# Step sizes, first norm and last block of a two-layer trunk: three changes of order in one kernel

## The chip, the cores and the metric

The kernel runs on one core of a Trainium2 chip. The metric is the device time of one execution in microseconds, the lower the better. The core has a matrix engine (PE, with its weight loads PEld), a vector engine (DVE), a scalar engine (ACT), a general engine (POOL) and a queue for transfers (SP). Each executes its own instructions in order and waits for others by semaphores.

## What is computed

The reference is a decoder trunk of two layers on 256 positions of width 2048, everything in float32:

```python
h = _mamba2_mixer(x, ...)              # layer 0
x = _layernorm(ALPHA * x + h, ln_g[0], ln_b[0])
k, v = _shared_kv(x, kv_w, kv_b, cos, sin)
h = _swa_mixer(x, k, v, ...)           # layer 1
x = _layernorm(ALPHA * x + h, ln_g[1], ln_b[1])
```

The mixer of layer 0 projects `x` to gates, values, B, C (8 groups) and step sizes (64 heads), convolves over time, and forms for each group decays `exp(-(sum of dt * a))`, which are multiplied into the products of C and B. The step sizes are `dt = softplus(dt_raw + bias)`, and the decays need their running sums over time. The outcome is gated, normalized by group and projected by `w_out`. Layer 1 is an attention over a window of 128 with one shared set of keys and values, projected from the normalized `x`; its own outcome is gated, projected by `w_out` and added to the normalized `x`, before the second norm.

## The kernel before, in words

**Weights.** All weights come in units of 128 x 2048 (`srcs`, the list of all of them in the order of use). A unit is loaded in two halves on SP's queue (`wr<-in_wa` and the like, L130) and each half is split into a high part (`wh`, ACT, L139) and the rest (`wl`, DVE, L140), so that a product in float32r of three matmuls gives float32's exactness: high by high, high by low, low by high (`mac`, L216; `out_unit`, L272; `x_stat`, L776). `next_unit` (L211) loads two units ahead of the one in use; there are four buffers each for the high and the low parts.

**Order.** A planner orders each engine's instructions at build time, from its own estimates of their durations and from the order in which the program issues them; `tc.keep_in_program_order(m)` takes the instruction `m` out of this freedom, and `tc.high_priority(n)` moves a stretch ahead. Work that belongs to a later step is called through `plan`, a list by step (`at(t, fn)`, ten steps for a group of layer 0), or in layer 1 through `later(n, fn)`, which calls it `n` ticks later; a tick follows each weight unit.

**Start.** `first_products` (L313) loads `x` transposed, unit 0 and the step sizes' weights in pieces (`FIRST`), and issues the products in the order of `ORDER`: entry 0 is the raw step sizes (L326, small float32 products), entries 1 and 2 are the products of units 0 and 1. `make_dt` (L338) then forms the step sizes in two functions. `first` (L344) has the bias, the absolute value and the exponential on ACT, and on DVE the reciprocal and the start of a polynomial for log(1 + e); `second` (L359) has eight polynomial steps (L362 to L364), `da = dt * a` and its rounding into a high and a low part (L368 to L371), two running sums (L374), and the transfer of the sums to a buffer in memory (`rscr`, L387). The calls are: load unit 2; `first`; load unit 3 with its DVE splits pinned; `second`; load unit 4 with its DVE splits pinned (L621 to L625). `turn_dt` (L393, step `TD`) transposes the sums. `load_decay` (L431) spreads rows of `rscr` over all partitions (`rb`), `sum_decay` (L451) subtracts and clips them on ACT into `e` (L459, eight operations for each half of a group), `exp_decay` (L464) applies the exponential, `by_cb` (L502) multiplies by the products of C and B on DVE. For group 0 the steps are `TS` for the first `sum_decay` and `TS + 1`, `TS + 2` for the rest.

**First norm.** `out_last` (L289) has the last group's output products (four blocks of 512 columns, two halves `h` of the positions), adds them to `xr` on DVE (L285) and takes statistics (L709). `done1(h)` (L726) follows each half: mean and variance (L713), Ln and Exp for the reciprocal deviation (L715, L716), and then for each chunk of 512 columns two operations on DVE (L731, L734) that also apply gain and shift from `gb`, spread over the partitions; four transposes of 128 on PE into one PSUM tile (L739); the high part `x1H` on ACT (L744), the low part `x1L` on DVE (L745). The keys and values (`x_stat`, L781 to L783) take `x1H` and `x1L`, chunk by chunk, for half 0 and then half 1.

**End.** The same `out_last` is used for layer 1 with `done2` (L977). For half 1 the second norm's last step is divided: for two chunks DVE subtracts the mean and multiplies by the gain (L992), PE adds the shift by a product of a row of ones with one row of the shift (L985) and multiplies by the reciprocal deviation as a diagonal matrix `dg` (L996), ACT copies and issues the transfer (L997, L998); for the other two DVE does both steps (L992, L1000) and SP issues the transfer.

Of the kernel before, what the change touches and what calls it, by code (L numbers as in the profile page):

```python
# [16 lines left out]
P = 128  # L17
# [11 lines left out]
TD, TS, CB0 = 3, 4, 8  # L29
# [3 lines left out]
ORDER = [(0, 0, 1), (1, 0, 2), (0, 1, 4), (1, 2, 6), (0, 4, 8), (1, 6, 8), (2, 0, 8), (0, 8, 14), (1, 8, 14),  # L33
         (0, 14, 16), (1, 14, 16), (2, 8, 16)]
# [12 lines left out]
           ("q", 3), ("g", 3), ("o", 2), ("o", 3)]  # L47
ALPHA = (2.0 * 2) ** 0.25
# [16 lines left out]
def trunk(ctx: ExitStack, tc: tile.TileContext, A: dict, out: bass.AP, dbg=None):  # L65
# [134 lines left out]
    def load_next(n, pin=False):  # L200
        for _ in range(n):
            if len(units) == 4:
                nc.sync.dma_start(cc[:], A["cc"])
            if len(units) in XK_AT:
                i = XK_AT.index(len(units))
                v = xr[:, i // 2, i % 2 * 1024 : i % 2 * 1024 + 1024]
                nc.sync.dma_start(v, A["xk"][:, i // 2, i % 2 * 1024 : i % 2 * 1024 + 1024])
                nc.scalar.activation(v, v, AF.Copy, scale=ALPHA)
            units.append(load_unit(srcs[len(units)], BROKEN if len(units) in broken else [WHOLE, WHOLE], pin))
# [62 lines left out]
    def out_unit(aH, aL, h, u, nb, first, rms=None):  # L272

        ps = mm_tile()
        hs = slice(h * P, (h + 1) * P)
        for k in range(4):
            ks = slice(k * 512, (k + 1) * 512)
            nc.tensor.matmul(ps[:], aH[:, k, hs], u.h[:, ks], start=k == 0, stop=False)  # L278
            nc.tensor.matmul(ps[:], aL[:, k, hs], u.h[:, ks], start=False, stop=False)  # L279
            nc.tensor.matmul(ps[:], aH[:, k, hs], u.l[:, ks], start=False, stop=k == 3)  # L280
        v = xr[:, h, nb * 512 : (nb + 1) * 512]
        if first:
            nc.vector.scalar_tensor_tensor(v, v, ALPHA, ps[:], ALU.mult, ALU.add)
        elif rms is not None:
            nc.vector.scalar_tensor_tensor(v, ps[:], rms[:, h : h + 1], v, ALU.mult, ALU.add)  # L285
        else:
            nc.vector.tensor_tensor(v, v, ps[:], ALU.add)

    def out_last(aH, aL, rms, stats, done):  # L289

        us = []
        for nb in range(4):
            us.append(next_unit())
            out_unit(aH, aL, 0, us[nb], nb, False, rms)
            stats(0, nb)
            if nb == 0:
                out_unit(aH, aL, 1, us[nb], nb, False, rms)
                stats(1, nb)
        done(0)
        for nb in range(1, 4):  # L300
            out_unit(aH, aL, 1, us[nb], nb, False, rms)
            stats(1, nb)
# [35 lines left out]
    def make_dt(ps):  # L338
# [3 lines left out]
        bias = pc[:, PC_DTB : PC_DTB + 1]  # L342

        def first():  # L344
            tc.keep_in_program_order(nc.vector.tensor_scalar(u, ps[:, :P], bias, None, ALU.add))
            nc.scalar.activation(e, ps[:, :P], AF.Abs, bias=bias)
            nc.scalar.activation(e, e, AF.Exp, scale=-1.0)
            aneg = ap.tile([P, 1], F32, tag="aneg", name="aneg")
# [7 lines left out]
            tc.keep_in_program_order(nc.vector.tensor_scalar(q, w, 1.0 / 15.0, None, ALU.mult))  # L356
            return aneg

        def second(aneg):  # L359
# [4 lines left out]
            tc.keep_in_program_order(ops.scalar_tensor_tensor(dt, u, 0.0, q, ALU.max, ALU.add))  # L364
            sums = f[4][:].rearrange("p (k t) -> p k t", k=2)
# [85 lines left out]
    def sum_decay(g, hf):  # L451
# [4 lines left out]
        for h in range(4):  # L456
            for c, cols in ((0, slice(0, 256)), (1, slice(256, 384))):

                nc.scalar.activation(  # L459
                    e[:, h, cols], rb[:, h, c * P :], AF.Relu, scale=-1.0, bias=rtk[:, c, h0 + h : h0 + h + 1]  # L460
                )
        es[g, hf] = e
# [158 lines left out]
    load_next(1)  # L621
    aneg = dt_first()
    load_next(1, True)
    dts = dt_second(aneg)
# [40 lines left out]
    for g in range(NG):  # L665
# [13 lines left out]
        else:  # L679
# [28 lines left out]
    def norm_stats(st, h, nb):  # L708
        nc.vector.bn_stats(st[:, h, nb, :], xr[:, h, nb * 512 : (nb + 1) * 512])  # L709

    def norm_scale(lp, st, h):
        mv = lp.tile([P, 2], F32, tag="mv", name=nm("mv"), bufs=2)
        nc.vector.bn_aggr(mv[:], st[:, h, :, :])  # L713
# [5 lines left out]
    with ExitStack() as s2:  # L719
        lp = pool("lp", stack=s2)  # L720
        gb = lp.tile([P, 2, D], F32, tag="gb", name="gb1")
        nc.gpsimd.dma_start(gb[:, 0, :], A["lng"][0].partition_broadcast(P))
        nc.gpsimd.dma_start(gb[:, 1, :], A["lnb"][0].partition_broadcast(P))
        st1 = lp.tile([P, 2, 4, 6], F32, tag="st", name="st1")

        def done1(h):  # L726
            mv, rs = norm_scale(lp, st1, h)
            for c in range(4):
                sl = slice(c * 512, (c + 1) * 512)
                t = lp.tile([P, 512], F32, tag="t", name=nm("t"), bufs=2)  # L730
                nc.vector.scalar_tensor_tensor(  # L731
                    t[:], xr[:, h, sl], mv[:, 0:1], gb[:, 0, sl], ALU.subtract, ALU.mult
                )
                nc.vector.scalar_tensor_tensor(  # L734
                    xr[:, h, sl], t[:], rs[:], gb[:, 1, sl], ALU.mult, ALU.add
                )
                ps = ax_tile()
                for k in range(4):
                    nc.tensor.transpose(  # L739
                        ps[:, k * P : (k + 1) * P], xr[:, h, c * 512 + k * P : c * 512 + (k + 1) * P], ident  # L740
                    )
                dst = (slice(None), slice(c * 4, c * 4 + 4), slice(h * P, (h + 1) * P))
                psv = ps[:].rearrange("p (k t) -> p k t", k=4)
                nc.scalar.activation(x1H[dst], psv, AF.Copy)  # L744
                nc.vector.tensor_tensor(x1L[dst], psv, x1H[dst].bitcast(F32), ALU.subtract)  # L745

        if PRE:
            tc.keep_in_program_order(nc.scalar.preload_act_table_set("natural_log_exp_and_others"))
        out_last(*gs[NG - 1].y, gs[NG - 1].rms, lambda h, nb: norm_stats(st1, h, nb), done1)
# [26 lines left out]
    def x_stat(ps, h, u, ui):  # L776
        for k in range(4):
# [3 lines left out]
            nc.tensor.matmul(ps[:], x1H[:, kk, hs], u.h[:, ks], start=kk == 0, stop=False)  # L781
            nc.tensor.matmul(ps[:], x1L[:, kk, hs], u.h[:, ks], start=False, stop=False)  # L782
            nc.tensor.matmul(ps[:], x1H[:, kk, hs], u.l[:, ks], start=False, stop=kk == KT - 1)  # L783
# [6 lines left out]
    for h in range(2):  # L790
        ps = mm_tile()
        for ui in range(4):
            if h == 0:
                kv_u.append(next_unit())
            x_stat(ps, h, kv_u[ui], ui)
# [17 lines left out]
        later(2, ktr)  # L813

# [160 lines left out]
    st2 = bp.tile([P, 2, 4, 6], F32, tag="st", name="st2")  # L975

    def done2(h):  # L977
        mv, rs = norm_scale(bp, st2, h)
        if h:

            dg = bp.tile([P, P], F32, tag="dg", name="dg")
            pss = [ax_tile(), ax_tile()]
            for c in range(2):
                sl = slice(c * 512, (c + 1) * 512)
                nc.tensor.matmul(pss[c][:], ones[0:1, :], gb2[1][0:1, sl], start=True, stop=False)  # L985
            nc.scalar.activation(dg[:], ident, AF.Copy, scale=rs[:])
            for c in range(4):
                sl = slice(c * 512, (c + 1) * 512)
                v = xr[:, h, sl]
                o = out[h * P : (h + 1) * P, sl]  # L990
                t = bp.tile([P, 512], F32, tag="pt", name=nm("t"), bufs=4)
                nc.vector.scalar_tensor_tensor(  # L992
                    t[:], v, mv[:, 0:1], gb2[0][:, sl], ALU.subtract, ALU.mult
                )
                if c < 2:
# [111 lines left out]
```

## Time and profile before

| | us |
|---|---|
| median of 3 runs | 1017.23 |
| lowest and highest | 1015.32, 1019.07 |
| the profiled execution | 1016.18 |
| its span in the trace | 1014.4 |
| PE, DVE, ACT busy | 999.1, 764.3, 558.5 |
| DVE splits of weights (L140) | 398.8 in 342 instructions |
| ACT splits of weights (L139) | 338.0 in 342 instructions |
| weights and other data moved | 198.79 MB |

An engine's busy time is the time in which one of its instructions ran. Matmuls overlap, and the profile models their ends, so for PE the distance from one start to the next is more telling than the busy time. A row of a timeline gives start, duration, engine, line, operation, output and input, and in brackets how long the engine was idle ahead of it and who ended that. A row of the table by stage gives a stretch and for each engine its busy time and number of instructions, then the granted clock of PE as a share, the share of the DMA engines and GB/s. A row of the waits gives the total, the number and the longest.

### The profile page before, as it was taken

What the parts mean: (1) busy time and instruction counts of PE and PEld (TensorE: products, weight loads), DVE (VectorE), ACT (ScalarE), POOL (GpSimd) and SP (SyncE); (2) the same over time, 40 slices, a digit from 0 to 9 for tenths busy, and PEclk for the clock granted to TensorE, in tenths of its full rate; (3) what the DMA queues carried; (4) which work ended last, traced back from release to release, by engine and by line L of the source; (5) the groups of instructions that cost most, each with busy time, mean ns of one, the idle gap of its engine ahead of it and who ended that gap; (6) DMA issues with size and microseconds to landing.
All of it is one profiled execution on the core that took longest, in us unless ns stands there. A gap on an engine that the chain in (4) does not pass through costs nothing.

```text
span 1014.4 us, 17615 instructions
## 1 busy us (share of the span) xinstructions
PE 999.1 (98%) x7011; PEld 900.2 (89%) x7011; DVE 764.3 (75%) x1109; ACT 558.5 (55%) x926; POOL 93.1 (9%) x116
## 2 busy tenths in 40 slices
PE   8999999999999999999999999999999999999997
PEld 7999899999998998999999999877988878879975
DVE  5679987877786787686786687798577775775786
ACT  5595847637655655664654764534554543543642
POOL 0100303004003002100300300401000000000002
PEclk9999999999999999999999999999999999999998
DMA  9896666575666666666656556646655545545532
GB/s 333 274 298 202 206 239 200 169 227 170 221 214 188 223 194 205 202 191 201 206 174 230 149 189 219 238 143 233 191 181 161 158 151 179 176 147 182 175 118 83
DMA packets 57858, 198.79 MB, mean 196 GB/s; under 512 B 6368, under 2 KB 10608, under 8 KB 57264
## 3 DMA queue, kind: packets, MB, share of 16 engines
q1 hardware_dynamic: 55648, 189.91, 57.9%
q0 software_dynamic: 1520, 7.10, 2.0%
q8 instruction: 55, 0.90, 0.4%
q10 hardware_dynamic: 608, 0.66, 0.2%
q14 instruction: 27, 0.22, 0.1%
HBM read 195.41 MB, written 2.23 MB: 195 GB/s over the span
## 4 chain that ended last, share of the span: by engine, by line
PE 82%; DVE 8%; ACT 3%; DMA 3%; issue 2%; POOL 1%; SPq 0%; ACTq 0%; POOLq 0%; DVEq 0%
PE mm L218 44%; PE mm L278 7%; PE mm L279 7%; PE mm L280 7%; PE mm L781 3%; PE mm L782 3%; PE mm L783 3%; DVE wl L140 2%; PE ax L537 2%; ACT wh L139 2%; PE ax L873 1%; PE ax L931 1%; DVE cv L419 1%; DMA wr<-in_wo 1%; DMA rb<-rscr 1%
## 5 line engine op out<-in xcount | busy, mean ns | idle before, releaser
L140 DVE TENSOR_TENSOR wl<-wr,wh 128x1024 fp32r<-128x1024 f32 (+2 forms) x342 | 398.8, 1183 | 135.7 <-ACT wh L139 133.8
L139 ACT ACTIVATE wh<-wr 128x1024 fp32r<-128x1024 f32 (+2 forms) x342 | 338.0, 1011 | 229.4 <-PE mm L218 74.3
L218 PE MATMUL mm<-xH,wh 128*128 128x256 f32 x1280 | 356.7, 279 | 1.7 <-DVE cv L419 1.3
L218 PE MATMUL mm<-xH,wl 128*128 128x256 f32 x1280 | 355.4, 278 | 1.3 <-DVE wl L140 1.3
L218 PE MATMUL mm<-xL,wh 128*128 128x256 f32 x1280 | 355.4, 278 | 0.0
L218 PEld LDWEIGHTS mm<-xH,wh 128*128 128x128 f32 x1280 | 241.2, 188 | 4.6 <-issue 2.4
L218 PEld LDWEIGHTS mm<-xH,wl 128*128 128x128 f32 x1280 | 241.1, 188 | 2.0 <-DVE wl L140 1.9
L218 PEld LDWEIGHTS mm<-xL,wh 128*128 128x128 f32 x1280 | 241.2, 188 | 1.0
L278 PE MATMUL mm<-wh,yH 128*128 128x512 f32 x256 | 101.4, 396 | 0.0
L279 PE MATMUL mm<-wh,yL 128*128 128x512 f32 x256 | 99.9, 390 | 0.0
L280 PE MATMUL mm<-wl,yH 128*128 128x512 f32 x256 | 99.7, 390 | 0.0
L553 POOL TENSOR_TENSOR yz<-yz,z 128x256 f32<-128x256 f32 x32 | 32.9, 1035 | 521.4 <-DVE yz L548 521.4
L419 DVE SCALAR_TENSOR_TENSOR cv<-mm,pc,cv 128x255 f32<-128x255 f32 x144 | 68.8, 478 | 8.3 <-ACT cv L417 6.9
L218 PE MATMUL mm<-x1H,wh 128*128 128x256 f32 x256 | 71.9, 281 | 0.0
L218 PE MATMUL mm<-x1H,wl 128*128 128x256 f32 x256 | 71.0, 277 | 0.0
L218 PE MATMUL mm<-x1L,wh 128*128 128x256 f32 x256 | 71.0, 277 | 0.0
L781 PE MATMUL mm<-wh,x1H 128*128 128x512 f32 x160 | 63.3, 396 | 0.0
L782 PE MATMUL mm<-wh,x1L 128*128 128x512 f32 x160 | 62.7, 392 | 0.2 <-DVE x1L L745 0.2
L783 PE MATMUL mm<-wl,x1H 128*128 128x512 f32 x160 | 62.6, 391 | 0.2 <-DVE wl L140 0.2
L278 PEld LDWEIGHTS mm<-wh,yH 128*128 128x128 f32 x256 | 48.1, 188 | 10.3 <-DVE z L490 1.0
L280 PEld LDWEIGHTS mm<-wl,yH 128*128 128x128 f32 x256 | 48.1, 188 | 10.2
L279 PEld LDWEIGHTS mm<-wh,yL 128*128 128x128 f32 x256 | 48.1, 188 | 9.0
(186 smaller groups left out, 1298.4 us busy)
## 6 DMA issues: line engine op xcount, KB each, us to landing
wr<-in_wa SPq DMA_DIRECT2D x158, 512.0 KB, 5.0
wr<-in_wo SPq DMA_DIRECT2D x64, 512.0 KB, 4.3
wr<-in_wq SPq DMA_DIRECT2D x32, 512.0 KB, 4.6
wr<-in_wg SPq DMA_DIRECT2D x32, 512.0 KB, 4.5
wr<-in_wb SPq DMA_DIRECT2D x32, 512.0 KB, 4.6
rb<-rscr SPq DMA_DIRECT2D x14, 512.0 KB, 5.1
wr<-in_wkv SPq DMA_DIRECT2D x8, 512.0 KB, 6.1
el<-rscr SPq DMA_DIRECT2D x14, 256.0 KB, 4.7
```

What stands on the lines that cost most here:

```text
L139: nc.scalar.activation(h[:, sl], v, AF.Copy)
L140: m = nc.vector.tensor_tensor(l[:, sl], v, h[:, sl].bitcast(F32), ALU.subtract)
L218: m = nc.tensor.matmul(ps, a, b, start=first and i == 0, stop=last and i == 2)
L278: nc.tensor.matmul(ps[:], aH[:, k, hs], u.h[:, ks], start=k == 0, stop=False)
L279: nc.tensor.matmul(ps[:], aL[:, k, hs], u.h[:, ks], start=False, stop=False)
L280: nc.tensor.matmul(ps[:], aH[:, k, hs], u.l[:, ks], start=False, stop=k == 3)
L419: nc.vector.scalar_tensor_tensor(a[:, sft:], ps[:, : S - sft], w(3 - sft), a[:, sft:], ALU.mult, ALU.add)
L537: nc.tensor.matmul(ps[64 * r : 64 * r + 64, cols], xd[:, c, r, :], e[:, 256:] if c else e[:, :256], start=c == 0, stop=c == 1,)
L553: nc.gpsimd.tensor_tensor(v, v, st.z[i][:], ALU.mult)
L781: nc.tensor.matmul(ps[:], x1H[:, kk, hs], u.h[:, ks], start=kk == 0, stop=False)
L782: nc.tensor.matmul(ps[:], x1L[:, kk, hs], u.h[:, ks], start=False, stop=False)
L783: nc.tensor.matmul(ps[:], x1H[:, kk, hs], u.l[:, ks], start=False, stop=kk == KT - 1)
```

## The change

1. **Step sizes.** In `ORDER` the small products of entry 0 from piece 8 to 16 come in one stretch, ahead of entry 1's; before, pieces 14 and 15 came in a second stretch. The chain is cut into three functions, with the DVE splits of units 2, 3 and 4, now all pinned, around them. The pins of the first function fall away. `TS` becomes 5. For groups 0 and 1 the `sum_decay` operations are pinned on ACT, the second half's `sum_decay` and `exp_decay` come one step later, and its `by_cb` as well. The loads of `xk` are pinned on SP's queue.
2. **First norm.** The norm is split: `center` subtracts the mean and divides by the deviation, alternating by chunk between DVE and ACT; the chunks are transposed, and gain and shift are applied after the transposition, where they are a column per partition (`gbc`, a new small input), four operations of 128 columns for each chunk, alternating between ACT and DVE. The transposes come in pairs of chunks, at fixed places in PE's order: half 0 among the last output products, half 1 among the keys' products. Output products and the keys' products of half 0 are pinned. Since `xr` now lacks gain and shift, `residual` applies them later, two DVE operations for each chunk and half, at ticks 1 to 4 and 9 to 12 of layer 1, with gain and shift loaded for each chunk.
3. **End.** In the last block of half 1 the product, the addition and the statistics come in two halves of 256 columns. The shift is added by a product of the identity with the shift spread over all partitions, and `dg` takes two and a half chunks in place of two.

```diff
-TD, TS, CB0 = 3, 4, 8
+TD, TS, CB0 = 3, 5, 8
-ORDER = [..., (2, 0, 8), (0, 8, 14), (1, 8, 14), (0, 14, 16), (1, 14, 16), (2, 8, 16)]
+ORDER = [..., (2, 0, 8), (0, 8, 16), (1, 8, 16), (2, 8, 16)]
+RES_AT = [1, 2, 3, 4, 9, 10, 11, 12]
...
-    load_next(1)
-    aneg = dt_first()
+    dt_first()
     load_next(1, True)
-    dts = dt_second(aneg)
+    dt_sums = dt_second()
+    load_next(1, True)
+    dts = dt_sums()
     load_next(1, True)
...
+        wide = g < 2
         at(steps, sum_decay, g, 0)
         at(steps + 1, exp_decay, g, 0)
-        at(steps + 1, sum_decay, g, 1)
-        at(steps + 2, exp_decay, g, 1)
+        at(steps + 1 + wide, sum_decay, g, 1)
+        at(steps + 2 + wide, exp_decay, g, 1)
         at(t + pos["cb"], cb, g)
         for hf in range(2):
-            at(t + pos["cb"] + hf * (g > 1), by_cb, g, hf)
+            at(t + pos["cb"] + hf, by_cb, g, hf)
...
+    def center(h):
+        mv, rs = norm_scale(lp, st1, h)
+        nmr = lp.tile([P, 1], F32, tag="nmr", name=nm("nmr"), bufs=2)
+        nc.vector.tensor_scalar(nmr[:], mv[:, 0:1], rs[:], -1.0, ALU.mult, ALU.mult)
+        for c in range(4):
+            v = xr[:, h, c * 512 : (c + 1) * 512]
+            if c % 2:
+                nc.scalar.activation(v, v, AF.Identity, scale=rs[:], bias=nmr[:])
+            else:
+                nc.vector.tensor_scalar(v, v, mv[:, 0:1], rs[:], ALU.subtract, ALU.mult)
+    def turn_x1(h, c, tp, tag, bufs):
+        ps = ax_tile()
...
+        for k in range(4):
+            v, g_, b_ = ps[:, k * P : (k + 1) * P], *[gbc[:, i, c * 4 + k : c * 4 + k + 1] for i in range(2)]
+            if c % 2:
+                nc.vector.tensor_scalar(x1[:, k, :], v, g_, b_, ALU.mult, ALU.add)
+            else:
+                nc.scalar.activation(x1[:, k, :], v, AF.Identity, scale=g_, bias=b_)
+        nc.scalar.activation(x1H[dst], x1, AF.Copy)
+        nc.vector.tensor_tensor(x1L[dst], x1, x1H[dst].bitcast(F32), ALU.subtract)
+    for h, nb in ((0, 0), (1, 0), (0, 1), (0, 2), (0, 3), (1, 1), (1, 2), (1, 3)):
+        if h == 0:
+            us[nb] = next_unit()
+        out_unit(*yHL, h, us[nb], nb, False, rms, True)
+        norm_stats(st1, h, nb)
+        if nb == 3:
+            center(h)
+        for c in {(1, 2): (0, 1), (1, 3): (2, 3)}.get((h, nb), ()):
+            turn_x1(0, c, x1p, "x1", 2)
...
+            x_stat(ps, h, kv_u[ui], ui, h == 0)
+            if h == 0:
+                for c in ((), (), (0, 1), (2, 3))[ui]:
+                    turn_x1(1, c, bp, "pt", 4)
...
+    def residual(c, h):
+        if h == 0:
+            for i, n in enumerate(("lng", "lnb")):
+                gb1[i] = bp.tile([P, 512], F32, tag=f"gb{i}", name=nm("gb1"), bufs=1)
+                nc.gpsimd.dma_start(gb1[i][:], A[n][0, c * 512 : (c + 1) * 512].partition_broadcast(P))
+        v = xr[:, h, c * 512 : (c + 1) * 512]
+        tc.keep_in_program_order(nc.vector.tensor_tensor(v, v, gb1[0][:], ALU.mult))
+        nc.vector.tensor_tensor(v, v, gb1[1][:], ALU.add)
...
-            pss = [ax_tile(), ax_tile()]
-                nc.tensor.matmul(pss[c][:], ones[0:1, :], gb2[1][0:1, sl], start=True, stop=False)
+            ends = (512, 512, 256, 0)
+            pss = [ax_tile()[:, :n] for n in ends[:3]]
+                nc.tensor.matmul(ps, ident, gb2[1][:, c * 512 : c * 512 + ends[c]], start=True, stop=False)
```

More of the change, by code (lines that the diff above doesn't have):

```diff
@@ L300, in out_last @@
         for nb in range(1, 4):
[L301 to L302 removed]
+            n = 256 if nb == 3 else 512
+            for c0 in range(0, 512, n):
+                out_unit(aH, aL, 1, us[nb], nb, False, None, False, c0, c0 + n)
+                stats(1, nb, c0, c0 + n)
         done(1)
@@ L717, in norm_scale @@
         return mv, rs
[L719 to L749, printed above, removed]
@@ L813, in trunk @@
         later(2, ktr)
+    def residual(c, h):
[6 more added lines that the diff above has]
+        nc.vector.tensor_tensor(v, v, gb1[1][:], ALU.add)
+    gb1 = {}
+    for c in range(4):
+        for h in range(2):
+            later(RES_AT[2 * c + h], lambda c=c, h=h: residual(c, h))
     qT = {}
```

122 lines of the change are left out of this document (76 added, 46 removed).

## The prediction

> **What bounds the kernel now.** I read the page first, for the engines' shares.
>
> ```profile
> span 1014.4 us, 17615 instructions
> PE 999.1 (98%) x7011; PEld 900.2 (89%) x7011; DVE 764.3 (75%) x1109; ACT 558.5 (55%) x926; POOL 93.1 (9%) x116
> ```
>
> PE is busy for 98% of the span, but ends of matmuls are modelled, so I look at how far apart matmuls start. The chain that ended last gives an undisturbed stretch of the 256-wide products and one of the transposes, and the timeline of PE the first and the last of 71 products 512 wide.
>
> ```profile
> 128.90 0.87 PE ax L514 x8
> ...
> 160.05 27.36 PE mm L218 x240
> ```
>
> ```profile
> 632.42 0.40 PE L279 MATMUL mm<-wh,yL 128*128 128x512 f32 x1
> ...
> 648.31 0.39 PE L280 MATMUL mm<-wl,yH 128*128 128x512 f32 x1
> ```
>
> A 256-wide product takes 27.36 / 240 = 0.114 us, a 512-wide one (648.31 - 632.42) / 70 = 0.227 us, a transpose 0.87 / 8 = 0.11 us. Almost all of the span is matmuls at this rate, which no part of the change alters. So the change can only gain where PE starts late. Groups 2 to 7 keep their order; for the stretch before them the timeline of PE shows:
>
> ```profile
> 36.14 0.28 PE L218 MATMUL mm<-xL,wh 128*128 128x256 f32 x1
> 36.99 0.39 PE L218 MATMUL mm<-xH,wl 128*128 128x256 f32 x1 [0.57 <-DVE wl L140]
> ...
> 59.09 0.28 PE L218 MATMUL mm<-xH,wl 128*128 128x256 f32 x1
> 59.70 0.39 PE L218 MATMUL mm<-xH,wh 128*128 128x256 f32 x1 [0.34 <-ACT wh L139]
> 59.92 0.28 PE L218 MATMUL mm<-xL,wh 128*128 128x256 f32 x1
> 60.96 0.39 PE L218 MATMUL mm<-xH,wl 128*128 128x256 f32 x1 [0.76 <-DVE wl L140]
> ...
> 121.46 0.39 PE L280 MATMUL mm<-wl,yH 128*128 128x512 f32 x1
> 123.20 0.36 PE L218 MATMUL mm<-xH,wh 128*128 128x256 f32 x1 [1.35 <-DVE cv L419]
> ```
>
> Start to start, less one product: 0.85 - 0.11 = 0.74, then 0.61 - 0.11 = 0.50 and 1.04 - 0.11 = 0.93, then 1.74 - 0.23 = 1.51 us. That is 3.7 us in reach of the first part.
>
> **Part 1, the step sizes' chain.** The timelines of PE, ACT and DVE show where it runs now, the chain that ended last and the waits of ACT what follows from it.
>
> ```profile
> 20.63 0.66 PE L326 MATMUL mm<-first 128*64 128x128 f32 x8
> ```
>
> ```profile
> 25.23 0.36 ACT L346 ACTIVATE f<-mm,pc 128x128 f32<-128x128 f32 x1
> ```
>
> ```profile
> 24.73 0.34 DVE L345 TENSOR_SCALAR f<-mm,pc 128x128 f32<-128x128 f32 x1
> ...
> 28.00 2.35 DVE L140 TENSOR_TENSOR wl<-wr,wh 128x1024 fp32r<-128x1024 f32 x2
> ...
> 35.72 2.36 DVE L140 TENSOR_TENSOR wl<-wr,wh 128x1024 fp32r<-128x1024 f32 x2
> ```
>
> ```profile
> 34.98 4.90 DMA rscr<-f
> ...
> 40.45 7.78 DMA rb<-rscr
> ```
>
> ```profile
> ACT e L459 <- DMA rb<-rscr: 4.8, 1, 4.8
> ```
>
> PE has the raw step sizes at 20.63 + 0.66 = 21.3, ACT takes them up only at 25.23. Between the splits of unit 3 (end 30.35) and of unit 4 (start 35.72) lie 5.4 us of chain in one run, and PE pays 0.74 for unit 4's late `wl`. The change cuts this run: 8 polynomial steps before unit 3's split, the rest before unit 4's. It also puts these last eight small products (pieces 14 and 15) ahead of the 18 of 256 columns that now precede them (pieces 8 to 13 of `ORDER`'s entry 1): 18 x 0.114 = 2.1 us earlier; with the run begun before unit 2's splits and not after them, I expect the chain 2 to 4 us earlier. No operation is added; 16 splits and chain steps only change places, and the splits are 2.4 us for a unit, less than half of the 48 x 0.114 = 5.5 us that PE spends on one. The 0.74 goes.
>
> Then `rb` lands earlier by as much, and the first `e` (L459) is planned one step of 5.5 us later. The two together cover the 4.8 us that ACT now stands behind `rb` with `cv` and `wh` queued behind it. That jam is what makes the splits late at 59: I count 0.50 + 0.93 as gone. On SP's queue the four loads of `xk` can no longer be drawn ahead of weight loads, so the DMA engines can carry less while `rb` is on its way; nobody waits for `xk` before the first addition to `xr` in group 1, and I count nothing for it. If the cover fails, the price is the present one. In group 1 the second half's eight `e` and its exponential come one step later, away from the splits; whether DVE's `cv` is then in time I can't see, so I count half of 1.51. Sum: 0.74 + 1.43 + 0.75 = **2.9 us gained**, between 0 (the waits only move) and 3.7.
>
> **Part 2, the first norm.** Timeline of PE for the stretch's ends, the table by stage for DVE, the groups of DVE in 650 to 700.
>
> ```profile
> 648.90 0.49 PE L278 MATMUL mm<-wh,yH 128*128 128x512 f32 x1
> ...
> 710.34 0.49 PE L808 MATMUL ax<-cc,kd 128*128 128x128 f32 x3
> ```
>
> ```profile
> 665.00:675.00 10.00, 9.59 (x51) 7.45 (x50) 9.85 (x15) 8.14 (x12) 1.07 (x2) 1.00 0.36 121
> 675.00:685.00 10.00, 9.49 (x41) 6.90 (x40) 10.00 (x15) 1.05 (x3) 0.00 (x0) 1.00 0.48 145
> ```
>
> ```profile
> L734 DVE SCALAR_TENSOR_TENSOR xr<-t,rs,gb 128x512 f32<-128x512 f32 x8 | 5.8, 744 | 0.0
> L731 DVE SCALAR_TENSOR_TENSOR t<-xr,mv,gb 128x512 f32<-128x512 f32 x8 | 5.7, 747 | 0.0
> ...
> L745 DVE TENSOR_TENSOR x1L<-ax,x1H 128x512 fp32r<-128x512 f32 x8 | 5.4, 686 | 0.2
> ```
>
> From the first output product of group 7 to the first transposes of the keys are 61.4 us. In them lie 96 output products and 144 of L781 to L783, 240 x 0.227 = 54.5, and 32 transposes, 3.5: 3.4 us are lost. The table shows by whom: DVE is at 9.85 and 10.00 of 10 us, ACT in the second row at 1.05. The change takes the 16 operations L731 and L734 from DVE, 16 x 0.745 = 11.9 us. It gives it 4 centerings (between 0.34, the 128-wide L345, and 0.75; I take 0.5: 2.0), 16 scalings of 128 out of PSUM (L345's 0.34: 5.4) and two tiny ones (0.4): 7.8. DVE wins 4.1 us, more than PE loses. ACT gets 4 centerings and 16 scalings:
>
> ```profile
> L459 ACT ACTIVATE e<-rb,rtk 128x128 f32<-128x128 f32 x64 | 24.9, 389 | 0.0
> ```
>
> 16 x 0.39 plus 4 x some 0.7 = 9 us, which its idle time in these rows holds. Transposes come in four pairs of chunks in place of single chunks; all 32 are fixed in PE's order, so PE waits there if a chunk isn't centered. Behind the first pair stand one product (12 x 0.227 = 2.7), a pair (0.9) and then the product that needs `x1L` of it: 3.6 us for four scalings (1.6), `x1H` (0.6) and `x1L` (0.69), which is 2.9 if no split of 1.2 (2.35 for two, above) comes between, and one mostly will. I leave 1.2 us lost: **2.2 gained**, between 3.4 and a loss of 1.2 (two splits at one pair).
>
> What is moved: `residual`, 16 operations of 512 on DVE (as L745, 0.69: 11 us), to the ticks of the first and second query block. The tight one is the second:
>
> ```profile
> 766.00:777.00 11.00, 11.00 (x66) 8.82 (x65) 8.72 (x19) 4.73 (x7) 0.54 (x1) 1.00 0.67 213
> ```
>
> DVE has 2.3 us free in this row and gets 2.8. Splits run up to two units ahead, so most is hidden: **0.4 lost**, between 0 and 2. The eight small loads of gain and shift go through POOL's queue, a step ahead of their readers.
>
> **Part 3, the end.** Timelines of DVE, PE and ACT, the page's list of DMA issues, the table by stage for the clock.
>
> ```profile
> 998.92 1.79 DVE L1007 SCALAR_TENSOR_TENSOR t<-xr,mv,gb 128x512 f32<-128x512 f32 x1
> ...
> 1003.33 0.69 DVE L287 TENSOR_TENSOR xr<-xr,mm 128x512 f32<-128x512 f32 x1
> ```
>
> ```profile
> 1003.23 1.98 PE L985 MATMUL ax<-gb,cc 1*128 1x512 f32 x4
> 1006.10 3.53 PE L996 MATMUL ax<-t,dg 128*128 128x512 f32 x4 [0.89 <-ACT dg L986]
> ```
>
> ```profile
> 1010.27 0.34 ACTq L998 DMA_DIRECT2D out<-xr  x1
> ```
>
> ```profile
> out<-xr ACTq DMA_DIRECT2D x2, 256.0 KB, 3.1
> ```
>
> ```profile
> 1002.00:1005.80 3.80, 3.20 (x10) 1.41 (x8) 3.59 (x7) 0.66 (x3) 2.34 (x2) 1.00 0.52 201
> 1005.80:1009.20 3.40, 3.10 (x4) 1.17 (x4) 3.40 (x6) 0.83 (x2) 0.00 (x0) 0.50 0.02 7
> ```
>
> ```profile
> L797 DVE TENSOR_TENSOR kd<-mm,bias 128x256 f32<-128x256 f32 x2 | 0.8, 420 | 0.0
> ```
>
> Halves gain nothing: DVE comes to the last block only at 1003.33, just when PE is done, because L1007 held it until 1000.7. Four operations of 0.42 + 0.03 in place of two of 0.72 are 0.3 more. Then the clock: it is 0.50 for most of L996, and the two chunks take 3.53 us in place of the 1.98 that the same width took in L985 at 1.00. Before that PE had only products of one row (1*128). With identity the shift is a product of 128 rows for 2.5 us, up to 1005.8, then 0.6 idle. If the clock stays, the three products with `dg` run from 1006.4 to 1008.9 (0.99 for a chunk), and ACT's copies and issues follow (0.58 + 0.38 each): last issue at 1009.8 in place of 1010.27, and the last transfer is half a chunk, which shortens its 3.1 us by something between 0 and 1.5; I take 0.3: **0.8 gained**. If it falls, PE ends at 1010.8 and 0.6 are lost.
>
> The Trainium skill, in "TensorE: Matmul & The Clock Gate", Part 1, says that the gate follows how busy PE was and halves the clock after an idle window of 3.4 us. By that rule products of one row are as busy as any; the trace disagrees, with PE busy for 3.20 of 3.80 us before the fall. It would make identity worthless, and is rival 2.
>
> **Sum.** 2.9 + 2.2 - 0.4 + 0.8 = 5.5 us. The profiled run took 1016.18 (span 1014.4 and 1.8 around it) and would come to 1010.7; it lies 1.05 below the median 1017.23, so I forecast 1017.23 - 5.5 = **1011.7 us**.
>
> **Rivals.** 1: both loaded engines clear wholly: 3.7 + 3.4 + 0.8 = 7.9, 1009.3. For it: DVE's 4.1 us. 2: the clock falls on idle time alone: 1.4 worse, 1013.1. For it: 0.6 us without a product remain. 3: the waits at the start only move, to ACT's later `e`: 2.9 less, 1014.6. For it: no work is taken away there. 4, the other side: the chain's first run stays where ACT has it now (25.23, done at 28.0), and the splits of unit 2, now fixed behind it, wait. PE wants them 30 products after the raw sizes, 21.3 + 3.4 = 24.7, and gets the first at 28.0 + 1.2: 4.5 us idle, long enough to halve the clock for a stretch as at 1005.80 (3.4 us, 1.7 lost). It costs from a first run that ends after 23.5 on; with 6.2 lost in place of 2.9 gained the sum is 3.6 slower, 1020.8 (1018 to 1024). Against it: the raw sizes are there at 21.3, so ACT's late start is one of order, and the change moves them earlier. 5: that the change doesn't do what it says is in 3.
>
> **Chances.** Forecast 0.42 (own range 1010 to 1013.5), rival 1 0.20, rival 2 0.10, rival 3 0.11, rival 4 0.17. A measurement of this kernel can tell some 0.5% (5.1 us) from no change: faster is below 1012.1, slower above 1022.3. Faster: two thirds of the forecast and rival 1, 0.48. Slower: over a half of rival 4, 0.10. Same: 0.42. The range leaves out half of rival 4 and the best of rival 1: 1007 to 1021.
>
> **What would show it.** Right: no gap of PE near 36 and 60, ACT not waiting for `rb`; under 2 us lost between L278's first product of group 7 and the keys' transposes; `dg`'s products at clock 1.00 and about 1 us each. Wrong: PE idle at 24 to 30; DVE still at 10 of 10 after 665 with PE waiting for `x1L`; PE waiting for `wl` in the second query block.

## The result, and the profile after

| | before | after |
|---|---|---|
| median of 14 runs, us | 1017.22 | 1013.5 |
| lowest and highest, us | 1015.32, 1019.07 | 1010.7, 1016.21 |
| the profiled execution, its span, us | 1016.18, 1014.4 | 1016.21, 1014.1 |

The ratio of after to before is 0.9962, with a 95% interval of 0.9951 to 0.9973: 3.9 us faster, 0.4%. That is less than the 0.5% from which the prediction would tell a change, so by its own bounds this counts as the same. The profiled execution of after is the longest of its 14, 2.7 us above the median, so the trace shows its faults larger than the median has them. The page's first rows look like before's:

```profile
span 1014.1 us, 17708 instructions
PE 1000.0 (99%) x7027; PEld 904.8 (89%) x7027; DVE 770.1 (76%) x1133; ACT 567.9 (56%) x947; POOL 102.2 (10%) x123
```

**The start.** First the table by stage of after; its columns are the stretch, the busy time and number of instructions of PE, PEld, DVE, ACT and POOL, the granted clock, the DMA share and GB/s.

```profile
44.00:56.00 12.00, 12.00 (x108) 12.00 (x107) 6.51 (x8) 5.12 (x6) 0.00 (x0) 1.00 1.03 330
56.00:62.00 6.00, 6.00 (x55) 6.00 (x55) 3.62 (x5) 3.43 (x5) 0.00 (x0) 1.00 0.98 376
62.00:68.00 6.00, 6.00 (x54) 5.95 (x53) 1.90 (x5) 6.00 (x14) 0.00 (x0) 1.00 0.71 261
...
94.00:98.00 4.00, 0.00 (x0) 0.00 (x0) 3.42 (x8) 1.61 (x3) 0.00 (x0) 0.92 0.66 212
98.00:102.00 4.00, 3.88 (x24) 2.73 (x26) 4.00 (x9) 2.09 (x5) 0.00 (x0) 0.50 0.31 125
```

PE is busy throughout 44 to 68, so the gap at 59 us is gone, as foreseen. But from 94 to 98 PE does nothing at all, and after that its clock is 0.50. The timelines of PE, first of before and then of after, show the place: group 0's `ymm`.

```profile
95.86 2.82 PE L537 MATMUL ax<-e,xd 128*64 128x256 f32 x32 [0.35 <-DVE xd L519]
```

```profile
93.34 0.28 PE L221 MATMUL mm<-xH,wl 128*128 128x256 f32 x1
98.12 5.39 PE L552 MATMUL ax<-e,xd 128*64 128x256 f32 x32 [4.50 <-DVE xd L534]
```

PE arrives earlier than before, at 93.6 instead of 95.5, and waits 4.50 us for `xd` in place of 0.35. The same 32 products then take 5.39 us instead of 2.82, because the granted clock is 0.50. The start's gain of some 2 us is spent here, and more.

**The norm.** The timeline of PE shows group 7's first output product and the first transposes of the keys.

```profile
652.67 0.49 PE L285 MATMUL mm<-wh,yH 128*128 128x512 f32 x1
...
711.71 1.03 PE L850 MATMUL ax<-cc,kd 128*128 128x128 f32 x8
```

The stretch is 711.71 - 652.67 = 59.04 us; before it was 710.34 - 648.90 = 61.44. That is 2.40 us gained. The table by stage answers to the rows of before:

```profile
665.00:675.00 10.00, 10.00 (x49) 8.36 (x49) 8.11 (x14) 6.25 (x12) 0.00 (x0) 1.00 0.28 81
675.00:685.00 10.00, 9.78 (x46) 7.58 (x45) 9.81 (x21) 8.36 (x15) 2.13 (x4) 1.00 0.78 232
766.00:777.00 11.00, 11.00 (x60) 8.65 (x59) 9.19 (x19) 7.73 (x18) 0.00 (x0) 1.00 0.44 136
```

The rows have the same times as before's, but in this trace the stretch begins 3.8 us later, so they hold nearly and not exactly the same work. DVE falls from 9.85 to 8.11 in the first row, and ACT rises from 1.05 to 8.36 in the second. In the third, the second query block, DVE goes from 8.72 to 9.19 and PE is busy for all 11 us, as before: `residual` costs PE nothing there.

**The end.** The timelines of PE and of ACT's queue, and the table by stage:

```profile
1003.71 2.31 PE L1042 MATMUL ax<-gb,cc 128*128 128x512 f32 x6
1006.71 2.42 PE L1054 MATMUL ax<-t,dg 128*128 128x512 f32 x6 [0.69 <-ACT dg L1043]
```

```profile
1009.53 0.87 ACTq L1056 DMA_DIRECT2D out<-xr  x2
```

```profile
1005.80:1009.20 3.40, 2.63 (x8) 1.06 (x6) 3.40 (x6) 1.67 (x5) 0.00 (x0) 1.00 0.16 61
```

The clock stays at 1.00 where it was 0.50 in before's trace, and two and a half chunks of `dg` take 2.42 us where two took 3.53. From the last output product's start to the span's end it was 1014.4 - 1002.91 = 11.5 us; now it is 1014.1 - 1003.59 = 10.5.

### The profile page after: what moved, and what is told of

It reads as the page before. It is cut to its first block, busy times and chain, and to the rows that moved or that the text cites. A ratio compares the mean times of both kernels' runs of the same rounds, so it can differ in the third digit from the quotient of the medians.

```text
span 1014.1 us, 17708 instructions
## 1 busy us (share of the span) xinstructions
PE 1000.0 (99%) x7027; PEld 904.8 (89%) x7027; DVE 770.1 (76%) x1133; ACT 567.9 (56%) x947; POOL 102.2 (10%) x123
## 4 chain that ended last, share of the span: by engine, by line
PE 88%; DVE 4%; DMA 3%; ACT 3%; issue 1%; SPq 0%; ACTq 0%; DVEq 0%
PE mm L221 45%; PE mm L285 8%; PE mm L286 8%; PE mm L287 8%; PE mm L820 3%; PE mm L821 3%; PE mm L822 3%; PE ax L552 2%; DMA xr<-in_xk 2%; DVE wl L141 2%; PE ax L930 1%; PE ax L988 1%; DMA wr<-in_wa 1%; ACT wh L140 1%; PE ax L970 1%
```

## The experiments

All kernels compute the whole of the reference. Each ratio is to the kernel before, run on the same chip; there its medians were 1016.3 to 1016.7 us. A ratio differs a little from the quotient of the medians.

**The three parts alone.** Each of three kernels has one numbered part of the change on top of before. The core of each edit:

```diff
# the start alone
+TD, TS, CB0 = 3, 5, 8
+    dt_first(); load_next(1, True); dt_sums = dt_second()
...
# the norm alone
+        for c in {(1, 2): (0, 1), (1, 3): (2, 3)}.get((h, nb), ()):
+            turn_x1(0, c, x1p, "x1", 2)
...
# the end alone
+            n = 256 if nb == 3 else 512
+                nc.tensor.matmul(ps, ident, gb2[1][:, c * 512 : c * 512 + ends[c]], start=True, stop=False)
```

The start alone. 

> The kernel before with the first part of the change alone (step sizes, TS 5, e pinned and spread, xk pinned). The forecast's step says 2.9 us faster than before. Theory (xk): the pinned xk loads are issued late, ACT stands behind the scaling of xr, and PE waits 2 to 5 us at group 0's products of e and xd near 95 us; that eats the 2.2 us won at 36 and 59 us, so this kernel is within 1 us of before, with a gap at 93 to 98 us that names xd. Rival (e): the same time and gap, since the pinned e are in this part as well; told apart by the run without the xk pin.

The norm alone. 

> The kernel before with the first norm and residual of the change alone. Forecast's step: 2.2 us won in the norm's stretch, 0.4 lost to residual. From the two traces: 2.4 won in the stretch from group 7's first output product to the keys' transposes, and 0.8 more after it. Expected 1.8 to 3.2 us faster than before.

The end alone. 

> The kernel before with the last block's halves and the identity shift alone. Forecast's step and the two traces agree: 0.8 us faster than before, with the clock at 1.00 while dg's products run. If the clock falls all the same: 0.6 slower.

| | median, us | ratio | 95% interval |
|---|---|---|---|
| before, on that chip | 1016.61 | | |
| start alone | 1017.2 | 1.0001 | 0.9986 to 1.0016 |
| norm alone | 1013.65 | 0.9963 | 0.9949 to 0.9976 |
| end alone | 1016.4 | 0.9986 | 0.9974 to 0.9998 |

The norm carries the gain, the start nothing. The end adds little: its interval goes from 0.2 to 2.6 us, and its median is only 0.2 us lower. In the start's kernel PE has one wait from 40 to 125 us, the same as in after:

```profile
PE ax L543 <- DVE xd L525: 4.7, 1, 4.7
```

So the new wait belongs to the start and needs no other part. What follows looks for its cause among the start's edits.

**The pins of `xk` off** (against after):

```diff
-                tc.keep_in_program_order(
-                    nc.sync.dma_start(v, A["xk"][:, i // 2, i % 2 * 1024 : i % 2 * 1024 + 1024])
-                )
+                nc.sync.dma_start(v, A["xk"][:, i // 2, i % 2 * 1024 : i % 2 * 1024 + 1024])
```

> The changed kernel without the pin on the four xk loads. Theory (xk): the first xk load goes out about ten loads earlier, ACT no longer stands behind xr, the gap near 95 us shrinks below 1.5 us and the clock isn't halved there: 1008.5 to 1011.5 us. Rival (e): the gap comes from the eight pinned e of each half ahead of cv on ACT and stays at 4 us or more: 1013 to 1014.

1013.48 us, ratio 0.996 (0.9939 to 0.998): the same as after. The wait is shorter but there, and the table by stage still has a halved clock:

```profile
PE ax L550 <- DVE xd L532: 2.9, 1, 2.9
```

```profile
96.00:100.00 4.00, 2.90 (x20) 2.05 (x22) 3.71 (x9) 2.60 (x4) 0.00 (x0) 0.57 0.55 183
```

Here PE also waits 1.4 us for `wl` at 82 us. The pin of `xk` alone is not the cause of the loss.

**The three edits of `e` undone** (against after):

```diff
-                if g < 2:
-                    tc.keep_in_program_order(m)
...
-        wide = g < 2
+        wide = 0
...
-            at(t + pos["cb"] + hf, by_cb, g, hf)
+            at(t + pos["cb"] + hf * (g > 1), by_cb, g, hf)
```

> The kernel after with the decay sums (e) of the first two groups no longer pinned to ACT's order and at the steps where the kernel before has them; the step sizes' chain and the pinned loads of xk as after. Theory E: the new wait of 4.5 us before group 0's ymm comes because sixteen additions of e stand in two closed blocks of 2.9 us on ACT at 62 and 73 us and hold up the products' cv there; then that wait shrinks below 1.5 us and the time falls to 1009 to 1011 us. Theory S (supply): whatever stands on ACT, the stretch from 44 to 62 us runs at the DMA's full share, so that an earlier PE only uses up its stock of weights and waits later; then about the same time is lost at another place between 60 and 100 us and the whole stays at 1012.5 to 1014.5 us.

1009.11 us, ratio 0.9931 (0.9918 to 0.9943), clear of after's interval. PE's wait ahead of `ymm` is 1.1 us, and its clock does not fall there. The theory of supply falls, and that of `e` stands. Two more kernels divide it.

**Only the pins of `e` off; only the later step taken back** (each against after):

```diff
# only the pins off
-                if g < 2:
-                    tc.keep_in_program_order(m)
...
# only the later step taken back
-        wide = g < 2
+        wide = 0
```

> The kernel after with only the pins of e taken off (groups 0 and 1); the second half's sum and exponential stay a step later than before, and so does the second half's by_cb. The kernel without all three edits of e took 1009.11 us against 1013.5. If the pins alone are the cause (they hold eight additions, 2.9 us, together on ACT where the products' cv could go between), this is 1009 to 1010 us, and the wait before group 0's ymm is at most 1.5 us. If the later steps are the cause (the second half's work falls together with the xr scalings and the silus of group 0's last blocks), it stays at 1012.5 to 1014, with the wait of 3 us or more.

> The kernel after with only the second half's sum and exponential of groups 0 and 1 put back to the steps that they have before; the pins of e stay, and by_cb stays a step later. If the pins alone are the cause this stays at 1012.5 to 1014 us, with two closed blocks of about 2.9 us of e on ACT and the wait before group 0's ymm of 3 us or more. If the later steps are the cause it is 1009 to 1010 us. If each is enough by itself, both this run and the one without pins stay above 1012.

Without the pins it is 1008.98 us, ratio 0.9928 (0.9911 to 0.9945); with the pins and without the later step 1011.93, ratio 0.9957 (0.9942 to 0.9972). The first is as expected. The second is not: it is under the 1012.5 expected, and the wait for `xd` is half of the 3 us. Its waits of PE are these, and the clock stays at 1.00:

```profile
PE ax L552 <- DVE xd L534: 1.5, 1, 1.5
PE mm L221 <- ACT wh L140: 1.5, 1, 1.5
PE mm L221 <- DVE wl L141: 0.9, 2, 0.8
```

So the pins lose some 3 us with the later step (0.9962 against 0.9928) and without it (0.9957 against 0.9931, where `by_cb` differs too); without it the loss comes in three kinds of wait in place of one. What the later step adds to the pins (0.9962 against 0.9957) is not to be told from nothing. ACT's timeline in after shows what a pin does (each row is eight additions of a half group):

```profile
62.30 2.86 ACT L472 ACTIVATE e<-rb,rtk 128x256 f32<-128x256 f32 x8
65.07 0.55 ACT L430 ACTIVATE cv<-mm,pc 128x256 f32<-128x256 f32 x1
...
73.39 2.87 ACT L472 ACTIVATE e<-rb,rtk 128x256 f32<-128x256 f32 x8
```

And without the pins:

```profile
45.38 0.51 ACT L472 ACTIVATE e<-rb,rtk 128x256 f32<-128x256 f32 x1 [3.86 <-DMA rb<-rscr]
...
48.83 1.78 ACT L472 ACTIVATE e<-rb,rtk 128x128 f32<-128x128 f32 x5
...
56.43 1.21 ACT L472 ACTIVATE e<-rb,rtk 128x256 f32<-128x256 f32 x3
...
57.83 1.79 ACT L472 ACTIVATE e<-rb,rtk 128x128 f32<-128x128 f32 x5
```

The same sixteen additions run from 45 to 60 us instead of 62 to 76. In that time ACT has room, since the DMA engines are at their full share and weights come no faster. The table by stage of the kernel without pins, against after's rows above:

```profile
44.00:56.00 12.00, 12.00 (x108) 12.00 (x107) 7.79 (x11) 10.62 (x18) 0.00 (x0) 1.00 1.01 311
56.00:62.00 6.00, 6.00 (x55) 6.00 (x54) 3.62 (x6) 6.00 (x14) 0.00 (x0) 1.00 0.98 351
62.00:68.00 6.00, 6.00 (x53) 5.95 (x52) 4.56 (x7) 5.90 (x7) 0.00 (x0) 1.00 0.99 361
```

ACT is busy for 10.62 of the 12 us from 44 to 56 in place of 5.12. From 62 to 68 it is full in both, but in after with additions, while DVE waits (1.90 us of work against 4.56) and the DMA engines too (0.71 against 0.99), which fits that the weights' splits, and so their buffers, come late. One row of DVE's timeline in after shows the wait:

```profile
65.65 1.52 DVE L432 SCALAR_TENSOR_TENSOR cv<-mm,pc,cv 128x255 f32<-128x255 f32 x3 [2.80 <-ACT cv L430]
```

DVE stands 2.80 us for the `cv` behind ACT's block of eight. In the 18 us that follow, 68 to 86, DVE is busy for 17.8 and can't make them good. Without the pins it also stands once behind a `cv`, 2.34 us at 61, but by then it has done more: 7.79 us of work against 6.51 from 44 to 56. The pins need not be all of it: in after ACT also stands 2.04 us behind a load of `xk` just ahead of the first block, at 59 to 61, and without the pins it doesn't. From ACT's first operation of the chain (20.27 us in after, 18.80 without the pins) to the start of `xd` (97.65 and 92.47) it is 77.4 us in after and 73.7 without the pins. (The profiled execution without the pins is 1.1 us below its median, so the two traces lie further apart than the medians.) In the kernel without pins PE gets it thus:

```profile
92.94 2.82 PE L550 MATMUL ax<-e,xd 128*64 128x256 f32 x32 [0.87 <-DVE xd L532]
```

**The scaling of `xr` moved to POOL** (against after, the pins of `e` on):

```diff
-                nc.scalar.activation(v, v, AF.Copy, scale=ALPHA)
+                nc.gpsimd.tensor_scalar(v, v, ALPHA, None, ALU.mult)
```

> The kernel after with the four scalings of xr (about 1 us each on ACT) on POOL, which has nothing to do from 45 to 100 us; they keep their place in program order. It takes 4.0 us of work and two waits of 2.0 us (for xk to land, at 82 to 87 us) off ACT just ahead of group 0's ymm. Theory A (ACT is what is late: it is busy for nearly all of 64 to 80 us and then stands behind xk): the wait before ymm falls from 4.5 us to under 1.5, the halved clock behind it goes, and the time falls by 3 to 5 us, to 1008.5 to 1010.5. Theory S (supply of weights): the wait only moves or stays, 1012.5 to 1014.5. Against both: if POOL's scaling takes DVE's port, DVE's operations beside it get longer and the time rises by up to 2 us.

1014.41 us, ratio 0.9975 (0.9964 to 0.9986): no gain. The wait for `xd` is 0.9 us shorter, and there is a new one; the clock falls here too. PE's waits:

```profile
PE ax L552 <- DVE xd L534: 3.6, 1, 3.6
PE mm L221 <- DVE wl L141: 1.2, 1, 1.2
```

Taking 4 us of work off ACT in this way does not help while the blocks of `e` stand where they are.

**The start of before with the norm and the end of after; then the pins of `e` added to it:**

```diff
# the second kernel, against the first
+                if g < 2:
+                    tc.keep_in_program_order(m)
```

> The kernel before with the norm's split and the last block in halves with the identity shift, but with the start of before (no pinned chain, e, xk or order of the first products). The norm alone gave 1013.65 us and the end alone 0.2 us, or 0.8 by its own profile. If the start is worth nothing in sum, this lies with the kernel after, 1012.5 to 1013.8 us; if the start's gaps at 36 and 59 us are a gain that lasts, this is 2 us slower than after, 1015 to 1016.

> The kernel with the start of before and the norm and end of after (1013.37 us), and added to it the pins of e alone, in groups 0 and 1, at the steps of before. With the start of after, taking the pins off gained 4.5 us (1008.98 against 1013.5). Theory E in its present form: the pins keep the sixteen additions out of ACT's idle time between 44 and 56 us, where the loads are the bound, and put them after 60, where each weight's split waits for ACT; the price is DVE's idle time behind ACT and comes with any start. Then this is 1015.5 to 1018 us. Rival: with the start of before, ACT stands behind rb at 45 us anyhow, so the additions already run in a closed block there and the pins change next to nothing: 1012.5 to 1014.5.

1013.37 us, ratio 0.9968 (0.9959 to 0.9978); with the pins 1012.64, ratio 0.9963 (0.995 to 0.9977). The first is level with after: the change's start is worth nothing in sum. The second was a miss for the theory of `e`: it expected the pins to cost 2 us or more with any start, and they cost none. Its profiled execution is the longest of its five, 2.8 us above the median. This trace has a wait of PE behind ACT (the first fence); without the pins PE waits elsewhere (the second):

```profile
PE mm L220 <- ACT wh L141: 3.1, 1, 3.1
PE mm L220 <- DVE wl L142: 1.3, 2, 0.8
PE ax L548 <- DVE xd L530: 0.9, 1, 0.9
```

```profile
PE mm L220 <- DVE wl L142: 2.1, 3, 0.8
PE mm L220 <- DVE cv L428: 1.3, 1, 1.3
PE ax L546 <- DVE xd L528: 0.8, 1, 0.8
PE mm L220 <- ACT wh L141: 0.3, 1, 0.3
```

A reading of why they are level comes from ACT's timeline without the pins:

```profile
48.42 1.20 ACT L468 ACTIVATE e<-rb,rtk 128x256 f32<-128x256 f32 x3 [6.38 <-DMA rb<-rscr]
```

With the old chain the free additions stand at the head of ACT's queue for 6.38 us and end that wait at 48.42. The pins remove that loss and put another of about its size in its place. With the new chain the free additions begin at 45.38, and then PE loses nothing at 59. By this reading the pins cost only where the place that they take the additions from had become free. It fits the traces; no run tests it by itself.

**The pins of `xk` off as well** (against the kernel with the three edits of `e` undone):

```diff
-                tc.keep_in_program_order(
-                    nc.sync.dma_start(v, A["xk"][:, i // 2, i % 2 * 1024 : i % 2 * 1024 + 1024])
-                )
+                nc.sync.dma_start(v, A["xk"][:, i // 2, i % 2 * 1024 : i % 2 * 1024 + 1024])
```

> The kernel without the three edits of e (1009.11 us) and besides without the pins of the loads of xk: what is left of the start's part is the step sizes' chain in three runs, the order of the first products and the move of the second load of decays by a step. The pin alone was worth nothing (1013.48 against 1013.5). If xk's place on SP matters only where ACT is late, this is the same as 1009.11 within 0.8 us; in the kernel without e's edits ACT waits 1.9 us for one landing of xk at 76 us and PE 2.4 us in all, so at the best it gains 1 us.

1013.8 us, ratio 0.997 (0.9958 to 0.9982): a miss as well, 4.7 us slower than expected. ACT's timeline and the long wait of PE:

```profile
72.70 1.06 ACT L209 ACTIVATE xr<-xr 128x1024 f32<-128x1024 f32 x1 [4.00 <-DMA xr<-in_xk]
73.66 0.40 ACT L433 ACTIVATE xs<-cv 128x256 f32<-128x256 f32 x1
```

```profile
PE ax L548 <- DVE xd L530: 3.2, 1, 3.2
```

Here ACT stands 4.00 us behind a load of `xk`, with a tanh that DVE needs queued behind the scaling; the outcome is again the wait for `xd`. It looks like the same fault with another instruction at the head. Whether it is SP's order itself or the planner's answer on ACT to it was not separated.

**The shift of the end by one-row products again** (against after):

```diff
-                nc.tensor.matmul(ps, ident, gb2[1][:, c * 512 : c * 512 + ends[c]], start=True, stop=False)
+                nc.tensor.matmul(ps, ones[0:1, :], gb2[1][0:1, c * 512 : c * 512 + ends[c]], start=True, stop=False)
```

> The kernel after with only the shift of the end put back to one-row products (ones times the first row of gb, as before), all else as after: the six products before the diagonal ones then use one row of the array in place of 128. If the clock fell in the kernel before because such products do not count as work, the granted clock at the diagonal products is 0.50 again, their 2.42 us become about 3.2 to 3.6, and the time rises by 0.6 to 1.2 us. If it fell because of the idle time alone, the clock stays at 1.00 as after, and the time moves by less than 0.3 us.

PE's timeline and the table by stage:

```profile
1001.31 2.41 PE L1042 MATMUL ax<-gb,cc 1*128 1x512 f32 x6
1004.22 3.35 PE L1054 MATMUL ax<-t,dg 128*128 128x512 f32 x6 [0.50 <-ACT dg L1043]
```

```profile
1006.00:1009.00 3.00, 1.56 (x3) 0.33 (x1) 1.07 (x3) 0.96 (x2) 0.00 (x0) 0.50 0.72 273
```

With the idle time ahead of `dg`'s products even shorter (0.50 against 0.69), the clock falls to 0.50 again, and they take 3.35 us instead of 2.42. Between this kernel and after only the number of rows differs. But two kernels above keep the end of before, and their traces speak against a simple rule. PE's timelines of the start alone and of the norm alone:

```profile
1008.48 1.98 PE L993 MATMUL ax<-gb,cc 1*128 1x512 f32 x4
1011.36 1.98 PE L1004 MATMUL ax<-t,dg 128*128 128x512 f32 x4 [0.89 <-ACT dg L994]
```

```profile
1004.30 1.98 PE L1046 MATMUL ax<-t,dg 128*128 128x512 f32 x4 [0.89 <-ACT dg L1036]
```

These are the same four one-row products as in before, with the same 0.89 us of idle time behind them, and the clock stays at 1.00: 1.98 us for two chunks in place of 3.53. In the traces kept, the clock fell in two of the four kernels with one-row products and in none of the ten with identity. That makes it likely that the rows have a part, but they do not decide alone; what else does, such as the moment at which the products come, was not separated.

The total does not follow the clock either: 1012.96 us, ratio 0.9968 (0.9958 to 0.9978), not to be told from after. From the last output product's start to the span's end it is 1011.8 - 1001.10 = 10.7 us here and 10.5 in after. With the end of before and the clock at 1.00 it is 1018.7 - 1008.17 = 10.5 in the start alone and 1012.1 - 1001.12 = 11.0 in the norm alone.

## Why the prediction came out as it did, step by step

The time of 1013.5 us lies in the range and in the forecast's own range, 1.8 us above the 1011.7. That it lies there, at the edge of the forecast's range, is in part luck: the first of the three terms gave nothing, and the measured values of the other two are larger than forecast, each with an interval that is wide against its size.

- **Part 1: 2.9 forecast, nothing measured** (start alone 1.0001; after against the kernel with the old start 0.9962 and 0.9968). The chain did move as described: its first ACT operation starts at 20.27 us in place of 25.23, PE has no gap at 36, 59 or 121, and ACT doesn't wait for `rb`. The step that failed is the one that took ACT's new order as a cover at no cost: "Then `rb` lands earlier by as much, and the first `e` (L459) is planned one step of 5.5 us later. The two together cover the 4.8 us that ACT now stands behind `rb`". The sum has no term for the pins that hold `e` on ACT. Without them, and with the later step still planned, the additions run from 45 us; it is the pins that put them after 62. Their later place was priced by what it avoids, not by what it meets: 2 x 2.9 us of additions put at 62 and 73 us, ahead of `cv` on an engine that has no room there, cost DVE 2.80 us in the trace, and DVE had no room to catch up. The runs show that the cover was not even needed: with the pins off, ACT stands 3.86 us behind `rb` and PE loses nothing at 59, for a total of 0.9928 against the old start's 0.9968, 0.4% or 4.1 us. That is the 2.9 foreseen or a little more; the change's own pins took it away. The half of 1.51 counted for group 1 was careful: the gap at 121 us is gone in after and without the pins, and it is there (1.3 us) in the kernel with all three edits of `e` undone.
- **Rival 3** (the waits at the start only move, to ACT's later `e`) describes what happened to this part, and its 1014.6 us is 1.1 above the result. It had the mechanism, with a chance of 0.11. The prediction looked at ACT by stage only in the norm and not between 60 and 80 us, where the additions would go. The cost of the clock was in no term of part 1 either: 5.39 - 2.82 = 2.6 us for these 32 products in the profiled execution.
- **`xk`** was counted at nothing. With `e` pinned that holds (0.996 against 0.9962). With `e` free its pins are worth 0.9931 against 0.997, 4 us; in the trace without them ACT's scaling waits 4.00 us for the load with others behind it. The sentence that nobody waits for `xk` before group 1 looked only at the reader of the result and not at the instruction in ACT's queue.
- **Part 2: 2.2 forecast, 2.4 in the trace**, and the norm alone gives 0.9963, 3.8 us (2.4 to 5.2). The sizes that I had to choose were a little small: a centering took 0.54 us on DVE and 0.81 on ACT (0.5 and 0.7 taken), a scaling 0.40 and 0.45 (0.34 and 0.39). They did not change the outcome: PE waits 0.2 us in this stretch in place of 1.1. Of the forecast loss of 0.4 by `residual` nothing was seen; from the keys' transposes to the last output product it is 291.88 us against 292.57, so this stretch gained 0.7 instead.
- **Part 3: 0.8 forecast, 0.9986 alone**, which is 1.4 us (0.2 to 2.6), with medians only 0.2 us apart. The traces of before and after give 1.0 (11.5 to 10.5 us), and the clock stayed at 1.00 as foreseen. But the prediction took the fall of the clock in the one trace of before for what always happens there. With the end of before and the clock at 1.00 the stretch takes 10.5 and 11.0 us, and in the ten traces with the new end 10.5 to 10.9. So these traces show a gain only where the clock would have fallen; how often it does was not measured.
- **Rival 2** (the clock falls on idle time alone) did not come: with 0.69 us idle it stayed at 1.00 in all ten traces with identity. What the prediction set against it, the rows, is not shown to decide. The Trainium skill, in "TensorE: Matmul & The Clock Gate", Part 1, says that the gate follows how busy PE has been. By the profile PE was busy for 3.20 of the 3.80 us that end 0.3 us ahead of `dg`'s products in before, where the clock fell, and for the same 3.20 of 3.80 in the start alone, where it stayed: busy time as the profile counts it does not tell the two apart.
- **Rival 4** did not come: the raw sizes are taken up at once, and PE has no wait at 24 to 30. **Rival 1** (both loaded engines clear wholly) did not come for the whole change, but the kernel without the pins of `e` is 0.9928, 7.3 us, against the 7.9 that it gave.

The best version found is after without the two lines that pin `e`: 1008.98 us, ratio 0.9928 (0.9911 to 0.9945), against 0.9962 (0.9951 to 0.9973).

## What to carry to other kernels

On an engine that works in order, a pin is a move, and it has two prices: what stands behind the instruction at its new place, and the idle time that is left unused at its old one. Read both from the table by stage at those two places, for the engine in question, and not from its share of the span; here ACT, at 56% of the span, was full from 62 to 68 us. Then look whether the engine that waits has room afterwards to catch up; here it hadn't, and a stall of 2.8 us of DVE was followed 30 us later by a wait of PE under another name. Two orders can also interact: with `xk` free the edits of `e` cost nothing (0.996 against 0.997), with `xk` pinned 3 us (0.9962 against 0.9931). So undo the pins one at a time and together. And before a loss at a place is put into a sum, look whether it is there in more than one trace.

## What the runs showed of the hardware

- **Waits of PE well under 3.4 us were followed by half the clock.** After a wait of 2.28 us, in the norm of the kernel with the start alone, the clock was 0.57 over the next 4 us (below). After 2.9 us (the run with the pins of `xk` off) it was 0.57 over 4 us, and after 4.50 us in after 0.50 over all of 98 to 102. After waits of 0.9, 1.1 and 1.5 us it stayed at 1.00. The Trainium skill, in "TensorE: Matmul & The Clock Gate", Part 1, gives an idle window of about 3.4 us as the condition; a wait a third shorter was enough here. It makes a wait dearer than it looks: with the 32 products behind it alone, 4.50 us of wait cost 7.1.

```profile
671.42 0.87 PE L747 MATMUL ax<-cc,xr 128*128 128x128 f32 x4 [2.28 <-DVE xr L742]
```

```profile
671.40:675.40 4.00, 3.98 (x13) 3.27 (x14) 4.00 (x6) 1.75 (x3) 0.00 (x0) 0.57 0.42 129
```

- **POOL is no cheap place for this scaling.** In the run with `xr` on POOL the four operations of 128x1024 took 2.8 to 3.9 us each by the profile, where ACT takes 1.06:

```profile
L211 POOL TENSOR_SCALAR xr<-xr x4: 2774/3345/3949, 58.4 to 82.1; 128x1024 f32<-128x1024 f32 x4
```
